# The last expert's rows written apart: down projection summed on top of the others in PSUM, output rows by an indirect write

## The chip, the cores and the metric

One core of one Trainium2 chip runs the whole program. The metric is the device time of one execution in microseconds, the median of three runs. A profile of one more execution gives the trace.

## The reference

Two stages. The first is two layers over x of 512 tokens by 1024 channels: an attention layer with forget gates and a gated recurrent layer, each followed by a gated projection. The second mixes tokens in three ways (long convolution, neighbourhood attention, pooling) and ends in a mixture of 16 experts and a last norm:

```
aff = softmax(rms_norm(x, norm2_g) @ w_router)            # 512 x 16
gate, idx = top_k(aff.T, 64)                              # each expert picks 64 tokens
y = (silu(xs @ w_gate) * (xs @ w_up)) @ w_down            # xs: the expert's 64 rows, w_*: 1024 x 2048 and back
x = x + zeros.at[idx].add(y * gate)                       # rows scattered back
return rms_norm(x, final_g)                               # 512 x 1024
```

All matrices are fp32. One expert has 24 MB of weights, the sixteen 403 MB. A token can be picked by several experts or by none.

## The kernel before

The first two thirds of the program are the layers up to the router. The change touches only the last part, `moe_body`, and two lines of `prepare`, which lays out the inputs.

**Weights.** `load` (L1493) issues the loads of one weight tile on SP's queue; a tile is 128 x 4096 fp32, 2 MB, and an expert has 12: four steps of gate and up (`mg`, `mu`, in the order `PARTS` = 0, 2, 1, 3) and four of down (`md`). `wtile` (L1481) hands out the places in turn; from expert 14 on the ring has eight, since the tile of the final gains, `FG`, keeps one for good. A load waits until the tile that had its place is used up. For expert 15 the last gate and up tiles come in two pieces, and the down tiles in four pieces of 512 KB each, rearranged so that a tile holds one half of the columns for two quarters of the rows (L1499 to L1507, runs of 2 KB in memory).

**One expert.** `gather` (L1575) builds a one-hot matrix from `rank` and multiplies it with `res` to get the expert's 64 rows. `up` (L1623) has eight steps (`at` 0 to 7, gate and up in turn) of eight matmuls each: 64 tokens on one half of PE's columns for one half of the channels, 64 on the other half. `issue_after(mm.ins)` puts what PE does for other purposes behind the step's last matmul on PE. Then the gate's Silu on ACT (L1652), the product with the up rows on DVE (L1653), eight transposes (L1662). `down` (L1668) makes the expert's output `Y` in one PSUM bank, 32 matmuls, and ACT copies it. `scat_mat` (L1611) builds the one-hot matrix times the gate values, transposed, and `scatter` (L1692) multiplies it with the copied rows and adds the result to `total` (512 x 1024, in SBUF), during the next expert's steps. For expert 15 the scatters of expert 14 come behind steps 0 to 3.

**The last expert.** Behind step 4 comes `scat_mat`, and behind steps 4 to 7 `base` (L1688), which puts the right half of `total`'s four token blocks into four PSUM banks by a matmul with the identity. After the transposes the down projection goes by `quarter` (L1738): four quarters for the left half of the columns, one for the right half, then the scatter matmuls of the left half (`add`, L1746) with their sums of squares and their product with the gains, then three quarters for the right half, and the scatter matmuls of the right half into the banks that hold `base`. For each of the four token blocks ACT sums the squares and takes the root, DVE takes the reciprocal (L1774) and the products (L1778, L1780), POOL scales the left half of three blocks (L1776), and SP writes the rows out (L1779 to L1784).

Tile's scheduler orders each engine's instructions by their order in the text and by when their inputs are ready in its model, and it adds all waits; also for two writes to the same rows of the output in memory.

Of the kernel before, what the change touches and what calls it, by code (L numbers as in the profile page):

```python
# [28 lines left out]
def _cols_layout():  # L29
    n = 0  # L30
    for name, w in (("pre0", 8), ("pre1", 8), ("post0", 8), ("post1", 8), ("lb0", 8), ("lb1", 8),
                    ("onorm", 1), ("norm1", 8), ("mix", 8), ("norm2", 8), ("norm2b", 8),
                    ("sw", 18), ("sb", 6), ("skip", 2), ("pscale", 2), ("freq", 1), ("fb1", 1),
                    ("fb2", 1), ("bf", 1)):
        COLS[name] = (n, w)
        n += w
    return n
# [17 lines left out]
def prepare(I):  # L55
# [6 lines left out]
    def pad(a):  # L62
# [15 lines left out]
        "fb2": pad(f["hy_f_b2_2"][0][:, None]), "bf": pad(f["att_b_f"][0][:, None]),  # L78
    }
# [120 lines left out]
class Kern:  # L200
# [1268 lines left out]
    def moe_body(self, R, out, mp):  # L1469
# [23 lines left out]
        def load(e, i):  # L1493


            n, i = SEQ[i]
            W[e, n, i] = w = wtile()
            src = I[n]
            if (e, n) == (15, "md"):  # L1499

                t = i // 2
                for r in range(2):
                    for kh in range(2):
                        nc.sync.dma_start(out=w.rearrange("p (r a k d) -> p r a k d", r=2, a=2, k=2)[:, r, kh],
                                          in_=bass.AP(tensor=src.tensor, ap=[[4096, 128], [1024, 2], [1, 512]],
                                                      offset=src.offset + (e * 2048 + (i % 2 + r * 2) * 512 + kh * 2) * 1024 + t * 512))
                return  # L1507
            if e == 15 and i == self.PARTS[-1]:

                for k in range(2):  # L1510
                    nc.sync.dma_start(out=w[:, k * 2048:k * 2048 + 2048],
                                      in_=bass.AP(tensor=src.tensor, ap=[[4096, 128], [1, 2048]],
                                                  offset=src.offset + (e * 4 + i) * 128 * 4096 + k * 2048))
                return
            nc.sync.dma_start(out=w, in_=bass.AP(tensor=src.tensor, ap=[[4096, 128], [1, 4096]],
                                                 offset=src.offset + (e * 4 + i) * 128 * 4096))

        def preload(e, k0, k1):
            for i in range(k0, k1):
                load(e, i)  # L1520

        def junk(name="junk"):
# [5 lines left out]
                      mx=(128, 4, 1), cnt=(128, 3, 4, 2), rank=(128, 4, 3), fin=(128, 4, 4, 1))  # L1528
# [94 lines left out]
        def up(e):  # L1623
# [5 lines left out]
            for at, (i, (n, A)) in enumerate(itertools.product(self.PARTS, (("mg", G), ("mu", U)))):  # L1629
# [38 lines left out]
        def down(e, hT):  # L1668
            Y = self.av("y")
            for i in range(4):  # L1670
                w = W.pop((e, "md", i)).rearrange("p (k d) -> p k d", k=4)
                for k in range(4):
                    kk = 4 * i + k
                    for t in range(2):
                        nc.tensor.matmul(Y[t * 64:t * 64 + 64, :], hT[:, i % 2 * 4 + k, i // 2, :], w[:, k, t * 512:t * 512 + 512],  # L1675
                                         start=kk == 0, stop=kk == 15, skip_group_check=True)
            YY[e] = y = Z[0][:, :512]
            nc.scalar.activation(y, Y, AF.Copy)

        P, FG = {}, []  # L1680

        def gains(t):
# [3 lines left out]
            nc.scalar.activation(fg[:, t * 512:t * 512 + 512], q, AF.Copy)  # L1686

        def base(i, p):  # L1688
            P[i] = p
            nc.tensor.matmul(p, self.ident, total[:, i, 512:], start=True, stop=False, skip_group_check=True)  # L1690
# [37 lines left out]

        e = 15
        preload(e, 0, NSEQ)  # L1730
        hT = up(e)
        fg = FG[0]
        fin, wo = tile_("fin"), wtile()
        wo = [wo[:, i * 1024:i * 1024 + 1024] for i in range(4)]
        nc.scalar.activation(fin[:, 0, 0:1], hT[:, 0, 0, 0:1], AF.Square)
        nc.scalar.activation(fin[:, 0, 0:1], fin[:, 0, 0:1], AF.Sqrt)

        def quarter(t, n, Y):  # L1738

            w = W[e, "md", t * 2 + n // 2].rearrange("p (r k d) -> p r k d", r=2, k=4)[:, n % 2]  # L1740
            for k in range(4):
                m = k % 2 * 64
                nc.tensor.matmul(Y[m:m + 64, :], hT[:, n // 2 * 4 + k, n % 2, :], w[:, k, :], start=n == 0 and k < 2,
                                 stop=n == 3 and k > 1, skip_group_check=True)

        def add(i, p, y, start):  # L1746
            nc.tensor.matmul(p, OHT[e][:, i * 128:i * 128 + 128], y, start=start, stop=True, skip_group_check=True)

        def sums(i, t, z):
            nc.scalar.activation(junk(), z, AF.Square, accum_out=fin[:, i, t:t + 1])  # L1750

        y = Z[0][:, :512], Z[0][:, 1024:1536]
        Y = [self.acc("y") for _ in range(2)]
        for n in range(4):
            quarter(0, n, Y[0])
        nc.scalar.activation(y[0], Y[0], AF.Copy)
        quarter(1, 0, Y[1])
        p = [self.acc() for _ in range(2)]
        for i in range(4):
            z = total[:, i, :512]  # L1760
            add(i, p[i % 2], y[0], True)
            V.tensor_add(z, z, p[i % 2])
            sums(i, 0, z)
            V.tensor_mul(wo[i][:, :512], z, fg[:, :512])
            V.tensor_scalar(fin[:, i, 2:3], fin[:, i, 0:1], 1.0 / D, EPS, op0=OP.mult, op1=OP.add)
        for n in range(1, 4):
            quarter(1, n, Y[1])
        nc.scalar.activation(y[1], Y[1], AF.Copy)
        for i in range(4):
            add(i, P[i], y[1], False)  # L1770
            sums(i, 1, P[i])
            f, w = fin[:, i, 3:4], wo[i]
            nc.scalar.activation(f, fin[:, i, 1:2], AF.Sqrt, bias=fin[:, i, 2:3], scale=1.0 / D)
            V.reciprocal(f, f)  # L1774
            if i < 3:
                nc.gpsimd.tensor_mul(w[:, :512], w[:, :512], f.to_broadcast([128, 512]))  # L1776
            else:
                V.tensor_scalar(w[:, :512], w[:, :512], f, None, op0=OP.mult)  # L1778
                nc.sync.dma_start(out=out[384:512, :512], in_=w[:, :512])  # L1779
            V.scalar_tensor_tensor(w[:, 512:1024], P[i], f, fg[:, 512:1024], op0=OP.mult, op1=OP.mult)  # L1780
            if i == 3:
                nc.sync.dma_start(out=out[384:512, 512:], in_=w[:, 512:1024])
            else:
                nc.sync.dma_start(out=out[i * 128:i * 128 + 128, :], in_=w[:, :1024])  # L1784
# [52 lines left out]
```

## Time and profile before

| | us |
|---|---|
| median of 3 runs | 1859.88 |
| lowest, highest | 1857.41, 1861.26 |
| the profiled execution | 1860.99 |
| its span in the trace | 1859.2 |
| PE busy | 1801.0 (97%) |
| DVE busy | 842.6 (45%) |
| ACT busy | 494.4 (27%) |
| POOL busy | 23.6 (1%) |

The span runs from the first to the last instruction of the trace; the program's own time is 1.8 us longer. PE is TensorE, DVE VectorE, ACT ScalarE, POOL GpSimd, SP SyncE. An fp32 matmul shows as two records. The ends of matmuls are modelled. A busy PE is therefore no proof that PE is the limit; the windows, the waits and the chain of what released what say which of PE, DMA and the small steps ends last in a stretch.

### The profile page before, as it was taken

The numbers are of one execution on the slowest core, as the hardware profiler recorded it, in microseconds if no ns is written. First come the engines' busy times: TensorE is split into PE (matmuls) and PEld (weight loads), VectorE is DVE, ScalarE is ACT, GpSimd is POOL, SyncE is SP. The second block draws the span as 40 slices with busy tenths as digits, with TensorE's granted clock in tenths as the row PEclk, the third lists the DMA queues.
The fourth block names the chain that finished last, engine by engine and source line by source line (L and its number), as shares of the span: only waits on it lengthen the run. The fifth ranks groups of instructions, "written<-read, shape, count | busy, mean of one in ns | idle before, by whom it ended". The sixth has DMA issues, their size and how long they took to land.

```text
span 1859.2 us, 21731 instructions
## 1 busy us (share of the span) xinstructions
PE 1801.0 (97%) x8656; PEld 1024.2 (55%) x8656; DVE 842.6 (45%) x1946; ACT 494.4 (27%) x869; POOL 23.6 (1%) x37
## 2 busy tenths in 40 slices
PE   9999999999999999999999999999999989999997
PEld 6767677888888888777733333333333333333332
DVE  6464767774635674777523222333213332133212
ACT  6453644463434454346301000000000000000002
POOL 0000000000000000000100000000000000000000
PEclk9999999999999999999999999999999999999999
DMA  4322233222121226335799999999999999999996
GB/s 166 114 80 83 77 122 130 100 94 98 57 80 57 102 102 219 120 112 193 305 385 420 414 428 427 428 427 428 427 428 427 427 427 428 428 427 427 428 424 225
DMA packets 61403, 496.94 MB, mean 267 GB/s; under 512 B 7161, under 2 KB 8313, under 8 KB 36459
## 3 DMA queue, kind: packets, MB, share of 16 engines
q1 hardware_dynamic: 51908, 470.46, 62.1%
q10 hardware_dynamic: 7592, 18.70, 2.9%
q0 software_dynamic: 1792, 6.29, 1.0%
q8 instruction: 70, 1.15, 0.2%
q14 instruction: 41, 0.34, 0.1%
HBM read 491.20 MB, written 4.23 MB: 266 GB/s over the span
## 4 chain that ended last, share of the span: by engine, by line
PE 76%; DMA 17%; DVE 5%; ACT 1%; issue 1%; SPq 0%; ACTq 0%; DVEq 0%
DMA w<-mu 15%; PE acc L337 11%; PE acc L338 11%; PE y L1675 11%; PE acc L339 11%; PE u L1635 8%; PE g L1635 6%; PE gx L1587 3%; PE st L1696 2%; DMA wraw<-wg 1%; PE hT L1662 1%; PE pt L637 1%; DVE wlo L306 1%; PE sc L333 1%; PE oT L803 1%
## 5 line engine op out<-in xcount | busy, mean ns | idle before, releaser
L337 PE MATMUL acc<-xhi,whi 128*128 128x512 f32 x800 | 318.1, 400 | 1.9 <-ACT xhi L323 1.8
L339 PE MATMUL acc<-xhi,wlo 128*128 128x512 f32 x800 | 314.2, 394 | 0.0
L1697 DVE TENSOR_TENSOR H<-H,st 128x512 f32<-128x512 f32 x120 | 78.1, 684 | 519.4 <-PE st L1696 519.4
L338 PE MATMUL acc<-xlo,whi 128*128 128x512 f32 x784 | 308.1, 393 | 0.2 <-DVE xlo L324 0.2
L1635 PE MATMUL g<-w,xt 128*64 128x512 f32 x1024 | 258.6, 595 | 10.5 <-DMA w<-mg 10.5
L1635 PE MATMUL u<-w,xt 128*64 128x512 f32 x1008 | 246.9, 596 | 8.5 <-DMA w<-mu 7.8
L306 DVE TENSOR_TENSOR wlo<-wraw,whi 128x1024 fp32r<-128x1024 f32 x127 | 155.2, 1223 | 183.9 <-ACT whi L305 165.6
L1675 PE MATMUL y<-w,ZH 128*64 128x512 f32 x944 | 222.9, 594 | 0.0
L305 ACT ACTIVATE whi<-wraw 128x1024 fp32r<-128x1024 f32 x127 | 134.3, 1057 | 212.5 <-PE acc L338 131.5
L337 PEld LDWEIGHTS acc<-xhi,whi 128*128 128x128 f32 x800 | 150.8, 189 | 38.5 <-issue 3.6
L1635 PEld LDWEIGHTS g<-w,xt 128*64 128x64 f32 x1024 | 78.7, 137 | 163.6 <-issue 134.0
L339 PEld LDWEIGHTS acc<-xhi,wlo 128*128 128x128 f32 x800 | 150.6, 188 | 31.1 <-issue 0.7
L338 PEld LDWEIGHTS acc<-xlo,whi 128*128 128x128 f32 x784 | 147.6, 188 | 32.3 <-issue 3.1
L1635 PEld LDWEIGHTS u<-w,xt 128*64 128x64 f32 x1008 | 74.1, 137 | 153.3 <-issue 130.1
L1675 PEld LDWEIGHTS y<-w,ZH 128*64 128x64 f32 x944 | 69.4, 137 | 130.4 <-issue 128.6
L1652 ACT ACTIVATE gs<-g 128x512 f32<-128x512 f32 x32 | 19.1, 597 | 405.1 <-PE g L1635 405.1
L1587 PE MATMUL gx<-res,oh 128*64 128x256 f32 x512 | 62.3, 385 | 10.8 <-DVE H L1697 10.8
L1619 ACT ACTIVATE ZH<-ogT 128x512 f32<-128x512 f32 x16 | 9.6, 598 | 229.2 <-PE ogT L1617 229.2
L1696 PE MATMUL st<-ZH 64*128 64x512 f32 x240 | 67.7, 641 | 0.0
L337 PE MATMUL acc<-whi,xhi 128*128 128x512 f32 x160 | 64.3, 403 | 0.0
L339 PE MATMUL acc<-whi,xlo 128*128 128x512 f32 x160 | 62.9, 393 | 0.0
L338 PE MATMUL acc<-wlo,xhi 128*128 128x512 f32 x160 | 62.9, 393 | 0.0
(520 smaller groups left out, 1928.9 us busy)
## 6 DMA issues: line engine op xcount, KB each, us to landing
w<-mg SPq DMA_DIRECT2D x63, 2048.0 KB, 33.2
w<-mu SPq DMA_DIRECT2D x62, 2048.0 KB, 31.9
w<-md SPq DMA_DIRECT2D x59, 2048.0 KB, 35.4
wraw<-wg SPq DMA_DIRECT2D x115, 512.0 KB, 3.5
w<-md SPq DMA_DIRECT2D x16, 512.0 KB, 10.8
cb<-cd ACTq DMA_DIRECT2D x16, 256.0 KB, 3.5
wraw<-wg POOLq DMA_DIRECT2D x8, 512.0 KB, 3.9
nab<-nab ACTq DMA_DIRECT2D x12, 256.0 KB, 2.6
```

The lines of the kernel that those rows point to most:

```text
L305: self.last = nc.scalar.activation(hi, w, AF.Copy)
L306: nc.vector.tensor_sub(lo, w, hi.bitcast(F32))
L333: mm(*a, skip_group_check=True, **k)
L337: mm(out, wh, xh, start=start, stop=False)
L338: mm(out, wh, xl, start=False, stop=False)
L339: mm(out, wl, xh, start=False, stop=stop)
L1587: nc.tensor.matmul(Q[w][t * 64:t * 64 + 64, :256], oh[:, i, :], rv[:, i, t, w], start=i == 0, stop=i == 3, skip_group_check=True)
L1635: mm = nc.tensor.matmul(A[b][t * 64:t * 64 + 64, :], xt[:, 2 * i + k, :], w[:, c:c + 512], start=at < 2 and k == 0, stop=at > 5 and k == 1 ...
L1652: nc.scalar.activation(g, G[b], AF.Silu)
L1675: nc.tensor.matmul(Y[t * 64:t * 64 + 64, :], hT[:, i % 2 * 4 + k, i // 2, :], w[:, k, t * 512:t * 512 + 512], start=kk == 0, stop=kk == 15 ...
L1696: nc.tensor.matmul(q, OHT[e][sl, i * 128:i * 128 + 128], YY[e][sl, :], start=True, stop=True)
L1697: V.tensor_add(total[:, i, t * 512:t * 512 + 512], total[:, i, t * 512:t * 512 + 512], q)
```

## The change

The output is now written twice. `rest`, called behind step 6 of expert 15, normalizes `total` as it stands after expert 14 (four squares on ACT, one root, a reciprocal, four products on DVE) and writes all 512 rows on SP's queue, behind the last weight load. The 64 rows that expert 15 picked are computed apart. `slot_rows` builds the one-hot matrix of expert 15 without the gate values and, by four small matmuls, each slot's gate value and token number. `base` gathers the picked rows of `total` into the PSUM bank `Y` by the same one-hot matrix. The gate value goes into the product of DVE (one factor more). The down projection is `down` as for the other experts, adding to what stands in `Y`, with channels 0 to 511 of the 64 rows on partitions 0 to 63 and the others on 64 to 127. A sum of squares of each partition, a matmul with `both` that adds the two halves of a row, root, reciprocal and products give the 64 rows, and POOL writes them by an indirect write of 128 half rows to the places in `idx`. `gains` copies the gains a second time in that layout. The down tiles of expert 15 have the layout of all the others, whole for the first three and in four pieces of runs of 4 KB for the last. The output's buffer `wo` is taken from the ring ahead of the down tiles. `cols` has five more columns (token numbers).

```diff
@@ prepare
+        "tok": np.concatenate([2.0 * np.arange(S).reshape(4, 128).T, np.arange(128)[:, None] // 64], 1).astype(np.float32),
@@ load
-            if (e, n) == (15, "md"):
-                t = i // 2
-                for r in range(2):
-                    for kh in range(2):
-                        nc.sync.dma_start(out=w.rearrange("p (r a k d) -> p r a k d", r=2, a=2, k=2)[:, r, kh],
...
-                return
-            if e == 15 and i == self.PARTS[-1]:
-                for k in range(2):
-                    nc.sync.dma_start(out=w[:, k * 2048:k * 2048 + 2048],
...
+            if e == 15 and i == (3 if n == "md" else self.PARTS[-1]):
+                m = 1024 if n == "md" else 2048
+                for k in range(0, 4096, m):
+                    early["last"] = nc.sync.dma_start(out=w[:, k:k + m], in_=bass.AP(tensor=src.tensor, ap=[[4096, 128], [1, m]],
+                                                      offset=src.offset + (e * 4 + i) * 128 * 4096 + k))
                 return
@@ up
-                    if e == 15 and at > 3:
-                        if at == 4:
-                            scat_mat(e)
-                        base(at - 4, (self.sc, self.sc, self.av, self.tp)[at - 4]("base"))
+                    if e == 15 and at == 4:
+                        slot_rows()
+                    if e == 15 and 4 < at < 7:
+                        base(2 * at - 10)
+                        base(2 * at - 9)
+                    if e == 15 and at == 6:
+                        rest()
...
-                V.tensor_mul(hh[:, b * 512:b * 512 + 512], g, U[b])
+                if e < 15:
+                    V.tensor_mul(hh[:, b * 512:b * 512 + 512], g, U[b])
+                else:
+                    V.scalar_tensor_tensor(hh[:, b * 512:b * 512 + 512], g, LAST["ai"][:, 0:1], U[b], op0=OP.mult, op1=OP.mult)
@@ down
-            Y = self.av("y")
+            Y = self.av("y") if e < 15 else LAST["Y"]
...
-                                         start=kk == 0, stop=kk == 15, skip_group_check=True)
+                                         start=kk == 0 and e < 15, stop=kk == 15, skip_group_check=True)
@@ gains
+            h = slice(t * 64, t * 64 + 64)
+            nc.scalar.activation(fg[h, 2048:2560], q[h, :], AF.Copy)
@@ new, in place of base, quarter, add, sums and the code that called them
+        def slot_rows():
+            og = Z[0][:, 512:1024].rearrange("p (i c) -> p i c", i=4)
+            for i in range(4):
+                V.tensor_scalar(og[:, i, :], self.slots, RANK[15][:, i:i + 1], None, op0=OP.is_equal)
+            at = tile_("at")
+            V.tensor_copy(at[:, :, 0], aff[:, :, 15])
+            V.tensor_copy(at[:, :, 1], self.col("tok", 0, 4))
+            q = self.tp("ai")
+            for i in range(4):
+                nc.tensor.matmul(q[:, 0:2], og[:, i, :], at[:, i, :], start=i == 0, stop=i == 3, skip_group_check=True)
+            ai = LAST["ai"] = tile_("ai")
+            V.tensor_copy(ai[:, 0:1], q[:, 0:1])
+            V.tensor_scalar(LAST["idx"], q[:, 1:2], self.col("tok", 4), None, op0=OP.add)
+            m = LAST["both"] = FG[0][:, 2560:2688]
+            V.tensor_add(m[:, :64], self.ident[:, :64], self.ident[:, 64:])
+            V.tensor_copy(m[:, 64:], m[:, :64])
+            LAST["og"], LAST["Y"] = og, self.av("y")
+
+        def base(i):
+            for t in range(2):
+                nc.tensor.matmul(LAST["Y"][t * 64:t * 64 + 64, :], LAST["og"][:, i, :64], total[:, i, t * 512:t * 512 + 512],
+                                 start=i == 0, stop=False, skip_group_check=True)
+
+        def rest():
+            fg, fin, wo = FG[0], tile_("fin"), LAST["wo"].rearrange("p (i c) -> p i c", i=4)
+            for i in range(4):
+                nc.scalar.activation(wo[:, i, :], total[:, i, :], AF.Square, accum_out=fin[:, i, 0:1])
+            nc.scalar.activation(fin[:, :, 1], fin[:, :, 0], AF.Sqrt, bias=self.eps, scale=1.0 / D)
+            nc.scalar.activation(fin[:, 0, 3:4], fin[:, 0, 1:2], AF.Silu)
+            V.reciprocal(fin[:, :, 2], fin[:, :, 1])
+            with self.tc.issue_after(early["last"].ins):
+                for i in range(4):
+                    V.scalar_tensor_tensor(wo[:, i, :], total[:, i, :], fin[:, i, 2:3], fg[:, :1024], op0=OP.mult, op1=OP.mult)
+                    nc.sync.dma_start(out=out[i * 128:i * 128 + 128, :], in_=wo[:, i, :])
@@ the end of moe_body
-        preload(e, 0, NSEQ)
+        preload(e, 0, 8)
+        LAST["wo"] = wtile()
+        preload(e, 8, NSEQ)
+        LAST["idx"] = mp.tile([128, 1], mybir.dt.int32, name="idx")
         hT = up(e)
...
+        y = tile_("fl")
+        nc.scalar.activation(y[:, 0:1], hT[:, 0, 0, 0:1], AF.Square)
+        nc.scalar.activation(y[:, 0:1], y[:, 0:1], AF.Sqrt)
+        down(e, hT)
+        Y, w = LAST["Y"], FG[0][:, 3072:3584]
+        nc.scalar.activation(junk(), Y, AF.Square, accum_out=y[:, 1:2])
+        V.tensor_mul(w, Y, FG[0][:, 2048:2560])
+        p = self.tp("both")
+        nc.tensor.matmul(p[:, 0:1], LAST["both"], y[:, 1:2], start=True, stop=True)
+        nc.scalar.activation(y[:, 2:3], p[:, 0:1], AF.Sqrt, bias=self.eps, scale=1.0 / D)
+        V.reciprocal(y[:, 3:4], y[:, 2:3])
+        V.tensor_scalar(w, w, y[:, 3:4], None, op0=OP.mult)
+        nc.gpsimd.indirect_dma_start(out=out.rearrange("s (t d) -> (s t) d", t=2), in_=w, in_offset=None,
+                                     out_offset=bass.IndirectOffsetOnAxis(ap=LAST["idx"][:, :1], axis=0))
```

## Rows read from the trace of the kernel before

**Rows 1.** The page: busy times, rate by slice, two groups, two DMA issues.
```profile
PE 1801.0 (97%) x8656; PEld 1024.2 (55%) x8656; DVE 842.6 (45%) x1946; ACT 494.4 (27%) x869; POOL 23.6 (1%) x37
...
GB/s 166 114 80 83 77 122 130 100 94 98 57 80 57 102 102 219 120 112 193 305 385 420 414 428 427 428 427 428 427 428 427 427 427 428 428 427 427 428 424 225
...
L305 ACT ACTIVATE whi<-wraw 128x1024 fp32r<-128x1024 f32 x127 | 134.3, 1057 | 212.5 <-PE acc L338 131.5
...
w<-md SPq DMA_DIRECT2D x59, 2048.0 KB, 35.4
...
wraw<-wg POOLq DMA_DIRECT2D x8, 512.0 KB, 3.9
```

**Rows 2.** Windows: length, busy (instructions) by engine, granted clock, DMA share, GB/s.
```profile
1820.00:1830.00 10.00, 9.70 (x48) 3.89 (x46) 2.67 (x4) 1.69 (x3) 0.00 (x0) 1.00 1.05 388
...
1850.00:1860.00 10.00, 0.00 (x0) 0.00 (x0) 0.14 (x1) 0.00 (x0) 0.00 (x0) 0.51 0.38 147
```

**Rows 3.** The chain that ended last, from 1804 us: start, length, what.
```profile
1804.48 3.58 PE g L1635 x16
1808.06 0.59 PE ogT L1617 x4
1808.65 0.86 PE base L1690 x2
...
1822.38 1.06 PE base L1690 x2
...
1824.69 7.95 PE y L1743 x36
...
1837.66 5.33 PE y L1743 x24
...
1843.01 0.61 ACT ZH L1768
...
1844.82 0.70 ACT junk L1750 x2
...
1845.54 0.30 ACT fin L1773
...
1845.87 0.17 DVE fin L1774
...
1849.40 0.74 DVE w L1780
```

**Rows 4.** DMA from 1800 to 1860 us: rate in slices of 1.5 us; SP's queue.
```profile
GB/s 415 421 399 431 426 411 401 400 404 305 350 385 391 388 389 389 388 381 385 392 384 296 220 168 86 19 5 0 0 11 0 11 336 380 392 300 18 5 5 0
...
q1 hardware_dynamic: 5706, 15.61, 67.3%
```

**Rows 5.** Groups by line, 1700 to 1860 us, columns as on the page.
```profile
L1736 ACT ACT_TABLE_LOAD x1 | 1.3, 1283 | 0.0
...
L1778 DVE TENSOR_SCALAR w<-w,fin 128x512 f32<-128x512 f32 x1 | 0.7, 708 | 0.0
```

**Rows 6.** Timeline of DVE: start, length, line, operation [idle before it].
```profile
1771.89 1.12 DVE L1614 TENSOR_SCALAR ZH<-slots,rank,aff 128x128 f32<-128x128 f32 x4 [0.57 <-PE ogT L1617]
...
1804.51 1.29 DVE L1697 TENSOR_TENSOR H<-H,st 128x512 f32<-128x512 f32 x2 [3.36 <-PE st L1696]
...
1821.63 0.69 DVE L1653 TENSOR_TENSOR ZH<-gs,u 128x512 f32<-128x512 f32 x1 [15.84 <-PE u L1635]
```

**Rows 7.** Timeline of ACT, columns as before.
```profile
1816.97 0.60 ACT L1652 ACTIVATE gs<-g 128x512 f32<-128x512 f32 x1 [7.69 <-PE g L1635]
```

**Rows 8.** Timeline of SP's queue: the last write.
```profile
1850.52 1.14 SPq L1782 DMA_DIRECT2D out_dram<-w  x1
```

**Rows 9.** Line L1782, the last write of 256 KB: issue to landing.
```profile
DMA to landing us min/median/max: 5.1/5.1/5.1
```

**Rows 10.** Line L1832, the program's end: SP's closing semaphores, first and last start.
```profile
L1832 SPq EVENT_SEMAPHORE  x14: 17/28/28, 1855.6 to 1859.1; - x14
```

**Rows 11.** DMA issues of the whole run: POOL's slowest group.
```profile
vw<-vd POOLq DMA_DIRECT2D x8, 256.0 KB, 12.5
```

More of the change, by code (lines that the diff above doesn't have):

```diff
@@ L33, in _cols_layout @@
                     ("sw", 18), ("sb", 6), ("skip", 2), ("pscale", 2), ("freq", 1), ("fb1", 1),
-                    ("fb2", 1), ("bf", 1)):
+                    ("fb2", 1), ("bf", 1), ("tok", 5)):
         COLS[name] = (n, w)
@@ L1498, in load @@
             src = I[n]
-            if (e, n) == (15, "md"):
-                t = i // 2
-                for r in range(2):
-                    for kh in range(2):
-                        nc.sync.dma_start(out=w.rearrange("p (r a k d) -> p r a k d", r=2, a=2, k=2)[:, r, kh],
-                                          in_=bass.AP(tensor=src.tensor, ap=[[4096, 128], [1024, 2], [1, 512]],
-                                                      offset=src.offset + (e * 2048 + (i % 2 + r * 2) * 512 + kh * 2) * 1024 + t * 512))
-                return
-            if e == 15 and i == self.PARTS[-1]:
-                for k in range(2):
-                    nc.sync.dma_start(out=w[:, k * 2048:k * 2048 + 2048],
-                                      in_=bass.AP(tensor=src.tensor, ap=[[4096, 128], [1, 2048]],
-                                                  offset=src.offset + (e * 4 + i) * 128 * 4096 + k * 2048))
+            if e == 15 and i == (3 if n == "md" else self.PARTS[-1]):
[3 more added lines that the diff above has]
+                                                      offset=src.offset + (e * 4 + i) * 128 * 4096 + k))
                 return
@@ L1527, in moe_body @@
                       **{f"w{i}": (128, 4096, 1) for i in range(self.WB)}, rtok=(128, 4, 1), rs=(128, 4, 1), aff=(128, 4, 16, 1),
-                      mx=(128, 4, 1), cnt=(128, 3, 4, 2), rank=(128, 4, 3), fin=(128, 4, 4, 1))
+                      mx=(128, 4, 1), cnt=(128, 3, 4, 2), rank=(128, 4, 3), fin=(128, 4, 4, 1), at=(128, 4, 2, 1), ai=(128, 1, 1), fl=(128, 4, 1))
         res = tile_("res")
@@ L1675, in down @@
                         nc.tensor.matmul(Y[t * 64:t * 64 + 64, :], hT[:, i % 2 * 4 + k, i // 2, :], w[:, k, t * 512:t * 512 + 512],
-                                         start=kk == 0, stop=kk == 15, skip_group_check=True)
-            YY[e] = y = Z[0][:, :512]
-            nc.scalar.activation(y, Y, AF.Copy)
-        P, FG = {}, []
+                                         start=kk == 0 and e < 15, stop=kk == 15, skip_group_check=True)
+            if e < 15:
+                YY[e] = y = Z[0][:, :512]
+                nc.scalar.activation(y, Y, AF.Copy)
+        LAST, FG = {}, []
         def gains(t):
@@ L1686, in gains @@
             nc.scalar.activation(fg[:, t * 512:t * 512 + 512], q, AF.Copy)
-        def base(i, p):
-            P[i] = p
-            nc.tensor.matmul(p, self.ident, total[:, i, 512:], start=True, stop=False, skip_group_check=True)
+            h = slice(t * 64, t * 64 + 64)
[17 more added lines that the diff above has]
+            LAST["og"], LAST["Y"] = og, self.av("y")
@@ L1729, in moe_body @@
         e = 15
-        preload(e, 0, NSEQ)
+        preload(e, 0, 8)
+        LAST["wo"] = wtile()
+        preload(e, 8, NSEQ)
+        LAST["idx"] = mp.tile([128, 1], mybir.dt.int32, name="idx")
         hT = up(e)
[L1732 to L1784, printed above, removed]
```

## The prediction

> **What bounds the kernel now.** I read the page first [rows 1]. PE is busy 97% of the span, but the rate row says more: from the middle on the core moves 427 GB/s slice after slice, which is the mixture of experts drawing its weights. Only the last slice is different, 225 GB/s. A change that touches the last expert alone can gain only there, so everything below is about the stretch from 1800 us to the end at 1859.2 us.
>
> The windows come next [rows 2]. In 1820 to 1830 both PE (9.70 of 10 us) and the DMA engines (1.05) are full. In 1850 to 1860 no engine computes but for 0.14 us, and the DMA share is 0.38: the output going out. So the end is a serial stretch behind the last weights.
>
> The chain of waits [rows 3] gives it step by step. PE runs without a gap through expert 15. The down projection begins at 1824.69 and its last matmul ends at 1842.98 (the row 1837.66 plus 5.33). Then: copy, scatter, sum of squares, root, reciprocal, products, up to the last product at 1849.40 plus 0.74 = 1850.14. SP issues the last write at 1850.5 [rows 8], it lands 5.1 us later [rows 9], at 1855.6, when SP's closing semaphores begin, and the program ends 3.6 us after that [rows 10]. The path is PE until 1842.98, 7.2 us of small steps, 5.5 us of writing, 3.6 us of ending.
>
> The transfers of this stretch [rows 4]: 15.61 MB on SP's queue after 1800, of which 2.10 MB are the output, so 13.51 MB of weights. The rate row (slices of 1.5 us) stays near 388 from 1817 to 1831 and fades by about 1837.
>
> **The change, part by part.**
>
> *PE before the down projection.* The old code puts four transposes and one identity matmul behind step 4 (0.59 + 0.86 us), and identity matmuls behind steps 5 and 6 (1.06 each, as the row at 1822.38): 3.57 us before step 7 begins. The new code puts four small matmuls (2 columns each) behind step 4 and four matmuls of the up projection's shape behind each of steps 5 and 6. The step at 1804.48 has eight of that shape in 3.58 us, so four cost 1.79. The small ones are not in the trace; the nearest row is the four transposes, 0.59, and they lie between 0.4 and 0.8; I take 0.59. Sum 4.17, so step 7 starts 0.6 us later. The fourth identity matmul (1822.38, 1.06 us) partly covers DVE's second product; without it the hidden transposes start some 0.2 earlier. The product takes a third operand, 0.74 (the last row of [rows 3]) for 0.69 (L1653, [rows 6]): 0.06 more. Down projection from 1824.69 + 0.45 = 1825.15.
>
> *PE in the down projection.* 32 matmuls of two records each in both versions. 36 records took 7.95 us, 0.221 each; 64 take 14.1, so the end is 1839.3 instead of 1842.98. Those 3.7 us are the scatter matmuls that no longer stand between the quarters.
>
> *Behind it.* Square with its accumulator 0.70 (1840.0), one 1-column matmul, not in the trace and between nothing and the 0.59 of four transposes, taken as 0.3 (1840.4), root 0.30, reciprocal 0.17, scaling of 128x512 at 0.71 [rows 5], with 0.1 of hand-overs: 1841.7. DVE's product with the gains runs beside the square. Before, the same stretch from the last matmul to the last product was 7.2 us; now it is 2.4.
>
> *The indirect write.* No row has one. Below, POOL's plain loads of 512 KB took 3.9 us from issue to landing [rows 1]; above, its slowest group, 256 KB each, 12.5 [rows 11]. I take 5.1: the 256 KB write of 2 KB rows from SP [rows 9] is the nearest in bytes and direction. In a sentence by itself: the Trainium skill, DMA: Bandwidth & Descriptors, section "Anatomy of one DMA", gives a DMA issued from GpSimd about 2.0 us fixed plus its bytes at 436 GB/s, which would be an estimate of 2.6 us here and an end 2.5 us earlier; the 3.9 us row for twice the bytes speaks more for a value above it. Landing 1841.7 + 5.1 = 1846.8, end 3.6 later: 1850.4.
>
> *The early output.* Four squares of 128x1024 on ACT (1.06 each by the row of L305, plus an accumulator read), a root and a Silu with a table load each (1.28, [rows 5]), then four products of 128x1024 on DVE, twice 0.75 each. DVE's last addition of expert 14 ends at 1805.8 [rows 6], ACT's next Silu is at 1816.97 after 7.69 us idle [rows 7]. From 1805.8: one square (the other three can go earlier), a table and the root end near 1808.7, with all four squares 1812.4; the second table frees ACT 1.5 later, by 1814 at worst; reciprocal and products end at 1815 to 1819, before DVE is wanted at 1821.6 for the hidden product. Cost nothing, with 3 us of cover at the least; if that is gone, see the last rival.
>
> *Queues.* On SP the four writes stand behind the last weight piece and nothing stands behind them. The output buffer is now taken ahead of the down tiles, so each of these loads waits for a buffer freed one step later (3.6 + 1.1 us). A 2 MB load lands 35 us after its issue [rows 1], so an issue 5 us later still meets 30 us of queued transfers: nothing lost. The down weights go whole again, as in experts 0 to 14 at 427 GB/s, against 388 in 2 KB runs: 13.51 MB are in by about 1833, at the old rate by 1835 and, with the old fading end, by 1838.7. PE wants the last quarter tile from 1835.7 and its last piece at 1838.4. So PE is not held. The writes follow: 15.61 MB at 412 (the mean of the first nine slices) is 1837.9, at 388 1840.2, plus an estimated 1 to 3 us to landing (below the 4.5 that the write of [rows 9] took beyond its own bytes, SP's issue among them): 1839 to 1843. This is the wait the change adds: POOL's indirect write overwrites rows of the same output and waits for all four landings; nothing is queued behind it but the ending. At 1841.7 the wait is about nothing; at the late end 1.3 us.
>
> Sum: 1859.2 to 1850.4, 8.8 us less: 3.68 from PE, 4.76 from the small steps, 0.38 from the write itself. The profiled run took 1860.99 us, 1.1 over the median 1859.88; from the median it gives 1851.1. With the bounds (indirect write 3.9 to 8, landing up to 1843) 1848 to 1854.
>
> **Rivals.**
>
> *The writes land late.* If the weights end as they did (1838.7) and 2.10 MB at 388 follow (5.4) with a landing of 1.5, the indirect write goes out at 1845.6 and all ends 3.9 us later: 1855. For it: the fading rate row shows engines ending 7 us apart. Against it: that fade followed sixteen pieces of 2 KB runs, which go. Chance 0.15.
>
> *The indirect write is dear.* 12.5 us to landing gives 1858.5, no change. For it: 128 row addresses have to be read and turned into descriptors by POOL, which has issued no such write before in this run. Against it: POOL's plain loads of twice the bytes land 3.9 us after issue [rows 1], with their descriptors made by the same engine. The Trainium skill, GPSIMD Engine Reference, section 2.1, says that the first call of a freshly loaded POOL routine pays some 6 us for its code; that would be an estimate of 1857, no change either, and no run here shows it. Chance 0.13.
>
> *ACT's queue holds the Silu.* One mechanism, and the slower side. If the four squares run only where the text has them, behind step 6 (1817.7), ACT is taken for 5.0 + 1.6 + 1.5 us and the Silus end at 1827; DVE's four products (6.0) stand ahead of the hidden product, so the down projection starts near 1833.6, 8.5 us late: 1859.6. PE would then idle, and where it idles at the end the granted clock is 0.51, against 1.00 in 1820 to 1830 [rows 2], 1.2 instead of 2.4 GHz; a down projection at half the clock costs up to 14 more: 1862 to 1873. It decides from 12.5 us of delay, start and clock together. Against it: the old kernel's one-hot rows for expert 15 (L1614) ran at 1771.89 [rows 6], 36 us before their place in the text, so ACT and DVE take work as it becomes ready. Chance 0.12, two thirds of it slower.
>
> **How the numbers follow.** Forecast 0.60 (1848 to 1854, all faster), late landing 0.15 (1853 to 1857, mostly faster), dear write 0.13 (same, with a little slower beyond 17.6 us), ACT's queue 0.12. A measurement of this kernel tells about 0.2%, 3.7 us, from no change: faster is below 1856.2. Faster 0.72, same 0.16, slower 0.12. Range 1847.5 to 1859: it leaves out the slow side of the last two rivals and a little below.
>
> **What would show it.** The down projection starts within 1 us of 1825 and ends near 1839 with no DMA wait; ACT's Silus of expert 15 still begin near 1817 to 1818; the four writes land before 1843; POOL's write is issued near 1842 and lands some 5 us later; 3.6 us of ending follow. A PE gap before the down projection, a POOL stretch over 8 us, or a DMA wait inside the down projection would make it wrong.

## The result and the profile after

The changed kernel takes 1847.85 us (median of 4 runs, 1847.72 to 1849.20), the kernel before beside it 1860.02: the medians lie 12.2 us apart, and the ratio, 0.9937 with a 95% interval of 0.9925 to 0.9949, stands for 11.7 us. The forecast was 1851.1, with a range of 1847.5 to 1859. The profiled execution took 1849.2 us, its span is 1847.0.

The page of the kernel after, its first row and the rate by slices:

```profile
PE 1792.5 (97%) x8654; PEld 1024.1 (55%) x8654; DVE 839.7 (45%) x1939; ACT 495.7 (27%) x863; POOL 21.8 (1%) x35
...
GB/s 168 114 81 86 75 118 128 101 99 95 65 80 57 96 88 219 132 117 172 286 403 403 421 426 428 427 428 427 428 427 428 427 427 428 428 427 429 427 427 323
```

Against [rows 1] the last slice changed most, 323 GB/s for 225: less of the end is spent without transfers.

The two spans can't be subtracted stage by stage from their beginnings. In the eleven traces of kernels that have the new program up to there, expert 0's first step already starts anywhere between 928.48 and 932.89 us, and expert 15's first step between 1780.55 and 1787.04. So each trace is read from that step on, and "the stretch" below is from there to the end of the span: 1785.47 to 1859.2, 73.73 us, before, and 1782.95 to 1847.0, 64.05, after.

The timeline of the kernel after, columns as in [rows 6]:

```profile
1782.95 4.02 PE L1628 MATMUL g<-w,xt 128*64 128x512 f32 x15
...
1803.31 1.06 ACT L1721 ACTIVATE w<-H 128x1024 f32<-128x1024 f32 x1 [3.50 <-DVE H L1735]
...
1805.47 1.05 PE L1702 MATMUL ai<-at,ZH 128*128 128x2 f32 x8
...
1807.81 3.67 DVE L1727 SCALAR_TENSOR_TENSOR w<-H,fin,w 128x1024 f32<-128x1024 f32 x3
...
1814.45 0.60 ACT L1648 ACTIVATE gs<-g 128x512 f32<-128x512 f32 x1 [6.86 <-PE g L1628]
...
1820.46 1.62 PE L1662 MATMUL hT<-ident,ZH 128*128 128x128 f32 x8
...
1822.01 7.09 PE L1675 MATMUL y<-w,ZH 128*64 128x512 f32 x32
...
1829.68 7.09 PE L1675 MATMUL y<-w,ZH 128*64 128x512 f32 x32 [0.58 <-DMA w<-md]
...
1836.81 0.60 ACT L1779 ACTIVATE junk<-y 128x512 f32<-128x512 f32 x1 [13.12 <-PE y L1675]
...
1837.55 0.38 PE L1782 MATMUL both<-fl,w 128*128 128x1 f32 x2 [0.79 <-ACT junk L1779]
...
1837.97 0.26 ACT L1783 ACTIVATE fl<-both,eps 128x1 f32<-128x1 f32 x1 [0.47 <-PE both L1782]
1838.27 0.16 DVE L1784 RECIPROCAL fl<-fl 128x1 f32<-128x1 f32 x1
1838.47 0.49 DVE L1785 TENSOR_SCALAR w<-w,fl 128x512 f32<-128x512 f32 x1
1840.47 1.04 POOL L1786 DMA_INDIRECT out_dram<-w,idx  x1 [927.16 <-DMA out_dram<-w]
```

The down projection is two rows of PE, 0.58 us apart: PE waited for the third down tile. Behind it stand five small steps, up to 1838.96; then nothing until POOL's write at 1840.47. The chain of waits says what that was:

```profile
1800.94 28.69 DMA w<-md
1829.63 0.02 issue
1829.65 0.02 SPq L1728
1829.67 0.03 issue
1829.70 9.84 DMA out_dram<-w
1839.53 0.03 POOLq L1786
```

It doesn't go through PE at all. It is the third down tile, then the last of the four early writes, which SP issued only when that tile had landed (issue at 1829.70, landing at 1839.53), and then POOL, which had waited for the write's landing. The write itself (line L1786 of the kernel after):

```profile
L1786 POOL DMA_INDIRECT out_dram<-w,idx x1: 1038/1038/1038, 1840.5 to 1840.5; - x1
...
DMA to landing us min/median/max: 5.0/5.0/5.0
```

The balance of the stretch, in us:

| part | before | after | forecast | measured |
|---|---|---|---|---|
| first step to the down projection's start | 39.22 | 39.06 | +0.45 | -0.16 |
| down projection | 18.29 | 14.76 | -4.13 | -3.53 |
| its end to the last product's end | 7.16 | 2.19 | -4.76 | -4.97 |
| to the last write's issue | 0.38 | 1.51 | 0 | +1.13 |
| issue to landing | 5.1 | 5.0 | -0.38 with the row above | -0.1 |
| landing to the end | 3.6 | 1.5 | 0 | -2.0 |
| sum | 73.7 | 64.05 | -8.8 | -9.7 |

(The forecast's down projection is its end at -3.68 less the later start.) The large terms came as forecast; two that stood at nothing, the wait for the early writes and the ending, did not.

### The profile page after: what moved, and what is told of

The parts are those of the page before. It is cut to its first block, busy times and chain, and to the rows that moved or that the text cites. A ratio compares the mean times of both kernels' runs of the same rounds, so it can differ in the third digit from the quotient of the medians.

```text
span 1847.0 us, 21691 instructions
## 1 busy us (share of the span) xinstructions
PE 1792.5 (97%) x8654; PEld 1024.1 (55%) x8654; DVE 839.7 (45%) x1939; ACT 495.7 (27%) x863; POOL 21.8 (1%) x35
## 4 chain that ended last, share of the span: by engine, by line
PE 75%; DMA 17%; DVE 5%; ACT 1%; issue 1%; ACTq 0%; POOLq 0%; SPq 0%; DVEq 0%
DMA w<-mu 11%; PE y L1675 11%; PE acc L339 11%; PE acc L340 11%; PE acc L341 10%; PE u L1628 8%; PE g L1628 7%; PE gx L1580 3%; PE st L1734 2%; DMA w<-mg 2%; DMA w<-md 2%; DMA wraw<-wg 1%; PE hT L1662 1%; PE pt L639 1%; PE sc L335 1%
## 5 line engine op out<-in xcount | busy, mean ns | idle before, releaser
L1675 PE MATMUL y<-w,ZH 128*64 128x512 f32 x1008 | 237.0, 595 | 0.6 <-DMA w<-md 0.6
L1675 PEld LDWEIGHTS y<-w,ZH 128*64 128x64 f32 x1008 | 73.9, 137 | 140.0 <-issue 136.6
```

## Experiments

Four questions: is the chip's scatter small enough to read these terms (r1); is the last stretch bound by PE or by weights (r2 to r4); why did the ending shrink by 2 us, a change nobody made (r5, r9, r6); what does the indirect write cost (r6 to r8, r10 to r12). All ratios are against the kernel before; a stretch is read from one trace of each kernel.

**The new kernel again (r1_new_again).** No edit.

> The changed kernel once more, for its spread. In the first trace of it expert 15's first step began at 1783.5 us against 1786.1 in the kernel before, although nothing in the program differs ahead of it but five columns of a constant. Theory A (that 2.5 us is chance from run to run): this trace puts the step anywhere from 1783 to 1787, and the median lies between 1847 and 1850.5. Theory B (the change moved the whole front): 1783.5 again within 0.3, median 1847.8.

Measured: 1849.52 us, ratio 0.9940 (0.9926 to 0.9953), stretch 63.66. Expert 15's first step came 0.7 us later than in the first trace (1783.64 for 1782.95) and the median 1.7 higher, within what theory A allowed and outside theory B. The stretch repeats within 0.4 us.

**Without the gather into PSUM (r2_no_gather_into_psum).**

```diff
                     if e == 15 and 4 < at < 7:
-                        base(2 * at - 10)
-                        base(2 * at - 9)
+                        pass
...
-                                         start=kk == 0 and e < 15, stop=kk == 15, skip_group_check=True)
+                                         start=kk == 0, stop=kk == 15, skip_group_check=True)
```

> The eight matmuls that gather total's rows into Y are left out (so the 64 rows lack the other experts' sum). Theory A (weights bound: PE stood 0.6 us before the third down tile, which landed at 1829.6): the down projection starts some 3.8 us earlier, waits that much longer for the third tile, and the time stays within 1 us of the changed kernel. Theory B (PE bound, as the prediction's sum had it): 3.8 us less, about 1844.

Measured: 1848.48 us, 0.9936 (0.9923 to 0.9950), stretch 63.18. PE of r2 around the down projection, timeline:

```profile
1815.40 1.62 PE L1661 MATMUL hT<-ident,ZH 128*128 128x128 f32 x8
...
1818.33 3.65 PE L1674 MATMUL y<-w,ZH 128*64 128x512 f32 x16 [1.31 <-DMA w<-md]
...
1823.25 3.65 PE L1674 MATMUL y<-w,ZH 128*64 128x512 f32 x16 [1.26 <-DMA w<-md]
...
1828.05 7.09 PE L1674 MATMUL y<-w,ZH 128*64 128x512 f32 x32 [1.14 <-DMA w<-md]
```

The transposes end at 1817.02, 35.7 us behind the first step (1781.32) for 39.1 in the kernel after: PE is ready 3.4 us earlier. Then it waits 1.31 + 1.26 + 1.14 us for tiles; the down projection ends at 1835.14, 53.8 us behind the first step, as in the kernel after (1836.77 less 1782.95). So a PE that is 3.4 us earlier brings nothing there: the weights set the end of the down projection, and in the change PE has just as much to do as the weights leave it time for.

**The third tile in pieces (r3_third_tile_in_pieces)**, and **all four in 2 KB runs (r4_down_in_2k_runs).**

```diff
r3
-            if e == 15 and i == (3 if n == "md" else self.PARTS[-1]):
+            if e == 15 and (n == "md" and i > 1 or n != "md" and i == self.PARTS[-1]):
r4
+            if e == 15 and n == "md":
+                for k in range(2):
+                    for t in range(2):
+                        early["last"] = nc.sync.dma_start(out=w.rearrange("p (k t d) -> p k t d", k=4, t=2)[:, 2 * k:2 * k + 2, t],
+                            in_=bass.AP(tensor=src.tensor, ap=[[4096, 128], [1024, 2], [1, 512]],
+                                        offset=src.offset + (e * 4 + i) * 128 * 4096 + k * 2048 + t * 512))
+                return
```

> The third down tile also comes in four pieces of 512 KB with runs of 4 KB. Theory A (the wait of 0.6 us before that tile is there because it counts only when the whole 2 MB are in): the wait goes, the down projection ends 0.6 us earlier, time 0 to 0.6 us less, as POOL then waits for the early writes. Theory B (the bytes themselves are late): no gain, or up to 1 us more since shorter runs are slower.

> The down tiles of expert 15 come in pieces with runs of 2 KB again, as in the kernel before (8 MB at 388 instead of 427 GB/s). Prediction's own step: down weights not on the path, so 0 to 1 us more. Rival (weights bound): 8.4 MB at 388 instead of 427 end 2.0 us later, the fading of the rate as before adds to it, PE waits, and POOL's write goes after later early writes: 2 to 4 us more, 1850 to 1852.

Measured: r3 1848.66 us, 0.9936 (0.9923 to 0.9950), stretch 64.16, down projection over at 54.5 us behind the first step, no gain for the finer grain: the bytes are late, not their signal. r4 1851.06, 0.9944 (0.9930 to 0.9958), stretch 64.98, down projection over at 55.1. The old form of the transfers costs the new kernel 0.9 us of the stretch against the first trace and 1.3 against r1, and 1.5 of r1's median, whose interval overlaps r4's: between the two expectations, so by the traces the whole tiles were a part of the gain, and a small one.

**The old kernel with its last writes from ACT (r5_old_last_write_from_act)**, and **with no write from SP (r9_old_no_writes_from_sp).** SP's program is over only when its last issue is; the idea is that SP's own closing instructions then stand on the path.

```diff
r5, r9
-                nc.sync.dma_start(out=out[384:512, :512], in_=w[:, :512])
+                nc.scalar.dma_start(out=out[384:512, :512], in_=w[:, :512])
...
-                nc.sync.dma_start(out=out[384:512, 512:], in_=w[:, 512:1024])
+                nc.scalar.dma_start(out=out[384:512, 512:], in_=w[:, 512:1024])
r9 alone
-                nc.sync.dma_start(out=out[i * 128:i * 128 + 128, :], in_=w[:, :1024])
+                nc.gpsimd.dma_start(out=out[i * 128:i * 128 + 128, :], in_=w[:, :1024])
```

> The kernel before, with the last two writes (256 KB each) issued by ACT instead of SP. In its trace SP branches out of the program at 1851.7, its first closing semaphore runs at 1855.6 without waiting and the next at 1857.6; in the changed kernel SP branches at 1830.1 and stands waiting at the end. Theory A (SP's own way to its closing code, not the landing, ends the kernel before): with ACT issuing, SP is at its closing semaphores in time and the program ends 1.5 to 3 us earlier, some 1.6 us after the landing. Theory B (the 3.6 us belong to what follows any last landing): no change within 0.5 us.

> The kernel before with none of the five output writes on SP: three blocks from POOL, the last block's two from ACT, so that SP's last issue is the last weight piece at about 1828. When ACT alone took the last two, SP still branched at 1849.5 and walked through its closing code until 1857.5 without a wait (a stop of 1.7 us in it), and nothing was gained. Theory A (SP's way to and through its closing code ends the kernel before): SP waits early, the program ends 1.6 us after the last landing, and the stretch from expert 15's first step to the end falls from 73.7 (73.1 with ACT) to 71 or 72. Theory B (what follows a last landing always takes 3.6): 73 or more, as POOL's issues come in between its products.

Measured: r5 1859.46 us, ratio 1.0000 (0.9991 to 1.0009); r9 1858.87, 0.9993 (0.9984 to 1.0002). Neither makes the old kernel measurably faster. What SP did is in the lines of its closing part: count, shortest, median and longest in ns, first and last start. The kernel before:

```profile
L1818 SPq COMPARE_BRANCH  x1: 46/46/46, 1851.7 to 1851.7; - x1
...
L1832 SPq EVENT_SEMAPHORE  x13: 17/28/28, 1857.6 to 1859.1; - x13
```

The kernel after:

```profile
L1821 SPq COMPARE_BRANCH  x1: 46/46/46, 1830.1 to 1830.1; - x1
...
L1835 SPq EVENT_SEMAPHORE  x14: 17/28/7132, 1835.3 to 1847.0; - x14
```

r5:

```profile
L1818 SPq COMPARE_BRANCH  x1: 46/46/46, 1849.5 to 1849.5; - x1
...
L1832 SPq EVENT_SEMAPHORE  x14: 17/28/28, 1854.3 to 1857.5; - x14
```

r9:

```profile
L1818 SPq COMPARE_BRANCH  x1: 46/46/46, 1829.8 to 1829.8; - x1
...
L1832 SPq EVENT_SEMAPHORE  x14: 17/28/22127, 1835.1 to 1859.1; - x14
```

In the kernel before SP branches out at 1851.7 and its first closing semaphore runs at 1855.6 [rows 10], 3.9 us later; the other 13 follow from 1857.6, and none waits (28 ns at most): the output had landed before SP was ready to look. After the change SP branches at 1830.1 and its closing instructions start at 1835.3, while PE still works; one of them waits 7.1 us (7132 ns) for the landing, and the end follows 1.5 us behind it. In r5 the last two issues went to ACT, but SP still issued the three blocks before, branched at 1849.5, and again none of its 14 waited: SP was as late as the output, and nothing measurable was won. In r9 SP was free 20 us early, one semaphore waited 22.1 us, and from the last product to the end it took 7.1 us instead of 9.06. POOL's issues stood between its products there, the last product came 0.96 later, and 1.0 of the 2.0 us was left, less than the median can show. So r9's trace and the kernel after show the cause of the shorter ending: SP is free before the last landing. The other kernels in which SP waits for the landing agree (r1, r7, r8, r10 to r12): they end 1.5 to 1.6 us after it, r9 1.9. r6 below limits it: there SP issues last again, and from the landing (1841.71 + 2.7) to the end at 1846.7 it takes 2.3 us, 0.8 more than in r7 and not 2. What the kernel before has and r6 lacks is a stop of 2.0 us within SP's closing part, between its first semaphore at 1855.6 [rows 10] and the next at 1857.6. What stops it there no run shows. In this stop lies one 8 KB transfer of queue q14, which the profile calls `instruction` (start 1856.10), and one lies in the stops of the kernel after (1835.83) and of r5 (1854.81) too, so a wait for SP's own code is the likeliest reading.

**The last write as a plain one, from SP (r6_sp_plain_last_write)**, **from POOL (r7_pool_plain_last_write)**, and **from POOL to the last rows (r11_pool_plain_to_last_rows).**

```diff
-        nc.gpsimd.indirect_dma_start(out=out.rearrange("s (t d) -> (s t) d", t=2), in_=w, in_offset=None,
-                                     out_offset=bass.IndirectOffsetOnAxis(ap=LAST["idx"][:, :1], axis=0))
r6
+        nc.sync.dma_start(out=out.rearrange("s (t d) -> (s t) d", t=2)[0:128, :], in_=w)
r7
+        nc.gpsimd.dma_start(out=out.rearrange("s (t d) -> (s t) d", t=2)[0:128, :], in_=w)
r11
+        nc.gpsimd.dma_start(out=out.rearrange("s (t d) -> (s t) d", t=2)[896:1024, :], in_=w)
```

> The changed kernel with the last 256 KB written by a plain write from SP to the first 64 rows instead of POOL's indirect write to the picked rows (so those rows are wrong). Theory A (SP's way to its closing code costs nearly 6 us after its last issue): SP issues at about 1840, and the end is no earlier than with POOL, 0 to 2 us later. Theory B (only landing counts, and SP's issue is quicker than POOL's): 1.5 us earlier than the changed kernel.

> The changed kernel with the last 256 KB written by a plain write from POOL to the first 64 rows (so those rows are wrong). Theory A (indirection costs little): issue to landing within 1 us of the 5.0 of the indirect write, time within 1 us. Theory B (reading the row numbers and making 128 descriptors is a large part of the 5.0): 2 us or more less.

> The changed kernel with a plain write from POOL to the last 64 rows, which belong to the early write that lands last (so these rows are wrong). The plain write to the first 64 rows did not wait for that landing, started 1.2 us earlier after expert 15's first step and landed in 2.6 us. Theory A (rows written a moment ago land slowly): it waits as the indirect write does, and lands in 3.4 to 5.0 us; the stretch from expert 15's first step to the end is 63 to 64 us. Theory B (indirection is the price): it waits, lands in 2.6 us, and the stretch is 61 to 62 us, against 60.4 to the first rows and 64.0 in the changed kernel.

**The indirect write to the first rows (r10_indirect_to_first_rows)**, and **the kernel without the four early writes (r8_no_early_write, r12_no_early_write_again).**

```diff
r10
-            V.tensor_scalar(LAST["idx"], q[:, 1:2], self.col("tok", 4), None, op0=OP.add)
+            V.scalar_tensor_tensor(LAST["idx"], self.col("tok", 4), -127.0, self.col("tok", 0), op0=OP.mult, op1=OP.add)
r8, r12
-                    nc.sync.dma_start(out=out[i * 128:i * 128 + 128, :], in_=wo[:, i, :])
```

> The changed kernel, but the indirect write goes to rows 0 to 63 whatever the router picked (so these rows are wrong). It still waits for all four early writes. Its landing took 3.4 to 5.0 us from issue in the kernels with early writes and 2.8 without them. Theory A (scattered rows that were written a moment ago land slowly): 3 us or less, as the rows of the first block have been in for some us. Theory B (an indirect write behind the early writes lands slowly wherever it goes): 3.4 to 5.0 again.

> The early write of the 512 rows is left out (only the 64 picked rows are written). Theory A (POOL waited for those writes, which landed 0.6 us after its data were ready, and 0.9 us of its own start follow): POOL's write starts 0.6 to 1 us earlier and the time falls by as much. Theory B (the early writes also slow the weights): the third down tile lands earlier too and 2 us or more go.

> The changed kernel without the early write of the 512 rows, once more. Its indirect write landed 2.8 us after issue; behind early writes six traces have 3.4 to 5.1, wherever it went, while plain writes there landed in 2.4 to 2.7. Theory A (an indirect write lands late only behind the early writes): 2.8 again within 0.4, and 60.6 us from expert 15's first step to the end, within 0.5. Theory B (the landing of an indirect write scatters by itself): 3.4 or more in this trace.

Measured, with the last write's issue counted from expert 15's first step:

| run | median us | ratio (95%) | issue at | issue to landing | stretch |
|---|---|---|---|---|---|
| after | 1847.85 | 0.9937 (0.9925 to 0.9949) | 57.5 | 5.0 | 64.05 |
| r10 | 1850.21 | 0.9952 (0.9935 to 0.9968) | 57.5 | 5.1 | 64.19 |
| r6 | 1847.10 | 0.9933 (0.9918 to 0.9948) | 56.0 | 2.7 | 61.0 |
| r7 | 1846.86 | 0.9935 (0.9920 to 0.9950) | 56.3 | 2.6 | 60.43 |
| r11 | 1847.62 | 0.9941 (0.9923 to 0.9959) | 57.2 | 2.4 | 61.1 |
| r8 | 1850.01 | 0.9949 (0.9934 to 0.9964) | 56.2 | 2.8 | 60.56 |
| r12 | 1846.59 | 0.9928 (0.9912 to 0.9945) | 56.6 | 2.8 | 60.95 |

r8 and r12 are one kernel on two chips: their medians differ by 3.4 us, their stretches by 0.4; r8's trace reached expert 15 at 1787.04, r12's at 1780.55. That is why the stretch is read here and not the median.

The landing of the last write, r12:

```profile
L1785 POOL DMA_INDIRECT out_dram<-w,idx x1: 1039/1039/1039, 1837.1 to 1837.1; - x1
...
DMA to landing us min/median/max: 2.8/2.8/2.8
```

r11:

```profile
L1786 POOL DMA_DIRECT2D out_dram<-w x1: 578/578/578, 1840.1 to 1840.1; - x1
...
DMA to landing us min/median/max: 2.4/2.4/2.4
```

r10:

```profile
L1786 POOL DMA_INDIRECT out_dram<-w,idx x1: 1041/1041/1041, 1839.6 to 1839.6; - x1
...
DMA to landing us min/median/max: 5.1/5.1/5.1
```

r8 fits neither of its theories: 3.1 to 3.5 us of the stretch went and not 0.6 to 1, and the third tile came no earlier, which theory B needed. r6's theory A fails: SP needed 3.0 us after its branch and not nearly 6.

An indirect write with nothing written before it lands 2.8 us after its issue, twice; where it has waited for the early writes 5.0, 4.6, 4.1, 3.4, 4.2 and 5.1 (after, r1 to r4, r10). A plain write of the same 256 KB takes 2.4 to 2.7 in the kernels with early writes. It is not the rows: r10 sends the indirect write to plain consecutive rows and pays 5.1, r11 writes plainly over the rows that were written last and pays 2.4.

The DMA queues show what stands in the way. POOL's writes go out on queue q0, in 80 packets; q8 has the kind `instruction`, which is program code, 16 KB a packet (queue: packets, MB, share of 16 engines). The kernel after, first from the issue at 1840.47 to 1843.93, then from there to the landing:

```profile
q0 software_dynamic: 75, 0.25, 18.4%
q8 instruction: 1, 0.02, 3.1%
...
q0 software_dynamic: 5, 0.02, 4.2%
```

then r12, first from the issue at 1837.11 to 1839.55, then from there to the end:

```profile
q0 software_dynamic: 80, 0.26, 28.1%
...
q8 instruction: 1, 0.02, 4.4%
```

In r12 all 80 packets have started before the code transfer. In the kernel after it comes among them, and the last five, a sixteenth of the write, start behind it. All traces of the new kernel and its variants in which POOL wrote last, with the first q8 transfer behind the issue, in us from the issue:

| run | code transfer starts | ends | last packet of the write starts | landing |
|---|---|---|---|---|
| r10, indirect | 1.70 | 3.64 | 4.63 | 5.1 |
| after, indirect | 1.79 | 3.49 | 4.48 | 5.0 |
| r1, indirect | 1.67 | 3.13 | 4.11 | 4.6 |
| r4, indirect | 1.74 | 2.79 | 3.77 | 4.2 |
| r2, indirect | 1.48 | 2.69 | 3.58 | 4.1 |
| r3, indirect | 0.52 | 1.92 | 2.91 | 3.4 |
| r8, indirect | 2.78 | 3.79 | 2.43 | 2.8 |
| r12, indirect | 2.45 | 3.81 | 2.43 | 2.8 |
| r7, plain | 2.94 | 4.00 | 2.14 | 2.6 |
| r11, plain | 2.08 | 3.26 | 2.07 | 2.4 |

The landing follows the last packet by 0.3 to 0.5 us in all ten. In the first six the code transfer is under way before the write is through, and the landing comes 1.4 to 1.5 us after its end; in the last four it starts when the last packet has gone. The code transfer starts 2.7 to 3.5 us after the last product in all of them. Without the early writes POOL issues 0.3 us after that product and is through in time; behind them it issues an indirect write 1.5 to 2.5 us after it and meets the code. The plain write of r11 escapes by 0.01 us, as its packets start 1.2 us after the issue, an indirect write's 1.6. So the lost 2.2 us go to a meeting with the loading of code, which the early writes bring about by holding the last write back. No run moves the code transfer by itself: this rests on the order and the times in the ten traces.

## Why the prediction came out

**PE before the down projection** (forecast 0.45 us later, measured 0.16 earlier). The extra matmuls behind steps 4 to 6 came as worked out in their sum: from step 4 to step 7 14.92 us for 14.31, +0.61 for 0.6. The parts were off and cancelled: by the distances of the steps, less the 3.58 of a step, the four small matmuls cost 1.0 us, above the 0.4 to 0.8 that they were put between, and the gather matmuls 1.6 each time for 1.79. The fourth identity matmul was undersized: taken as 0.2, it had held the transposes back by 0.9, and from step 7 to the down projection it is now 5.20 for 5.97 us.

**The down projection** (end 3.68 us earlier forecast; 3.69 from the first step, 0.16 + 3.53). That the size was right is luck: PE began 0.61 us earlier than forecast and then waited 0.58. "So PE is not held" failed by that wait, for the third tile; the forecast had held only the last tile against PE (and 13.51 MB at 427 GB/s are in by 1831.6, where it says about 1833). By its own list a DMA wait inside the down projection makes it wrong in this part. And r2 shows that the weights would have given the same end with PE 3.4 us earlier. The forecast had compared PE with the weights at 427 and 388 GB/s and taken PE as the later; the two are level.

**The small steps** (-4.76, measured -4.97). The five steps cost what their rows said; the scaling took 0.49 for the 0.71 of [rows 5].

**The early output** (nothing). ACT took the four squares at 1789.38, 1794.02, 1798.67 and 1803.31, as the blocks of the sum came ready; DVE's products ran between 1806.4 and 1811.5 and the gate's Silu at 1814.45 right behind its matmuls. The rival in which ACT's queue holds the Silu would have put the down projection 8.5 us late; it started 0.16 early. That rival is refuted.

**The writes land late.** In kind this rival came true, in size not: the last landed at 1839.53 instead of at 1845.6. The rival had the weights in at 1838.7; PE's last row of the down projection was over at 1836.77, without a wait for them behind the third tile. What the forecast's sum of bytes left out is that SP issued the last early write only at 1829.70, when the third tile had landed. POOL's wait behind the ready data cost 0.57 us, and its start 0.94 more from the landing to the issue: the +1.13 that the forecast put at "about nothing". r8 and r12 price the early writes altogether: the stretch is 3.1 to 3.5 us shorter without them than in the kernel after, of which 0.9 to 1.3 is the earlier issue and 2.2 the faster landing. They don't slow the weights: the third tile lands 46.6 and 47.0 us behind the first step without them, 46.7 with them.

**The indirect write** (5.1 chosen, measured 5.0). The number was right for a reason that doesn't hold: it was taken from SP's old last write [rows 9], which resembles it in bytes but stood behind 1.8 MB of other output, while r12 gives 2.8 for the write itself, and the other 2.2, by the traces, go to the code transfer that it met. That the two came to 5.0 is luck. The Trainium skill, DMA: Bandwidth & Descriptors, section "Anatomy of one DMA", would give an estimate of 2.6 us: r7's plain write (2.6) and r12's indirect one (2.8) agree, the kernel after (5.0) doesn't. The dear write of 12.5 us did not occur. POOL started 0.3 us after its data in r12. The Trainium skill, GPSIMD Engine Reference, section 2.1, puts some 6 us on the first call of a freshly loaded routine; this trace shows no such stretch at POOL's first indirect write.

**The ending** (3.6 taken over unchanged, measured 1.5). This is the largest miss, 2.0 us. [rows 10] had the sign of it: 14 closing semaphores of at most 28 ns, so none had waited for the write, and a landing at the very moment at which SP became free. The prediction read the two as cause and effect; it was two paths of about equal length, and with the last issue off SP the longer one is gone. This miss and the +1.13 above partly cancel, which brought the stretch's forecast, 8.8, nearer to the 9.7 than its terms were.

**What lies before.** The terms of the stretch give 9.7 us and the medians 12.2. In the profiled executions 2.5 us come from expert 15 starting earlier. Over all traces it starts at 1783.4 on the mean with the new front (eleven traces) and at 1785.5 with the old (three, 1784.51 to 1786.48). Most of that is the scatter of single executions; whether some 2 us are the change's own was not settled. The forecast lay 3.3 us above the measurement, 0.9 from the stretch and the rest from there.

## What to carry to other kernels

Read a program's ending for which engine is last to be free: closing instructions that never wait point to this engine, not the transfer, as what sets the end, and an earlier landing alone then brings little. When a small last write lands late, look at the queues of kind `instruction` between its issue and its landing before blaming its form. Where a stretch is bound by PE and by weights at once, sizing one of them says nothing about what its removal brings. When the front of a program scatters by more than the terms in question, compare from a common event near the change.

## What the hardware showed that was not expected

- SP needed 3.0 to 5.3 us from the branch that leaves its program to the first closing semaphore (r6 3.0, before 3.9, r5 4.8, after 5.2, r9 5.3). The first closing semaphore comes 1.3 to 1.5 us after the end of an 8 KB transfer of kind `instruction` in all five. Where SP issues last this lies on the path, in r6 too, whose closing part runs without a stop:

```profile
L1820 SPq COMPARE_BRANCH  x1: 41/41/41, 1842.1 to 1842.1; - x1
...
L1834 SPq EVENT_SEMAPHORE  x14: 17/28/28, 1845.1 to 1846.6; - x14
```

- A 16 KB transfer of program code started in all ten traces 2.7 to 3.5 us after the last product, before the last write was through in six of them; there the write landed 1.4 to 1.5 us after the code transfer's end, 3.4 to 5.1 us after its issue. Where the write was through first, it landed in 2.8 us (indirect) and in 2.4 to 2.6 (plain, from POOL).
